# First stage of a two-layer trunk: three products and the low-rank features side by side by k-tile, in place of one output after another

## The chip, the cores and the metric

The kernel runs on one core of a Trainium2 chip. The metric is device time in microseconds; the number compared is the median of several runs.

## The reference

A streaming encoder takes 256 frames of a prompt and 32 frames of a sample, 288 tokens of 2048 features in float32, through two layers. Layer 0 is a mix of retention heads and gated linear attention heads (GLA), layer 1 is band attention; each is followed by a convolutional feed-forward block. Only the very beginning matters here:

```python
h = rmsnorm(x, p['norm_mix_g'][l])          # x * gain / rms, the rms over 2048 features of a token
z = jnp.einsum('btd,de->bte', h, w_in)       # 56 x 128 outputs, and 16 more: lo
qa, ka, va, ga, qb, kb, vb, gb, lo = jnp.split(z, cuts, axis=-1)
...
log_a = jax.nn.log_sigmoid(lo @ gate_w2 + gate_b) / GLA_GATE_TAU
```

The first GLA head needs its key, query and values (parts of kb, qb, vb) and the gates, which come out of the 16 low-rank features lo.

## The kernel before, in words

Features lie on the 128 partitions and the 288 tokens along the free dimension; a k-tile is 128 of the 2048 input features, so there are 16. Each float32 operand is split in two parts of a shorter type (a high part, h, and the low remainder, l), and a product is three TensorE passes per k-tile: wh with xh (L79), wh with xl (L80), wl with xh (L81). One output tile of 128 features is therefore 48 matmuls of 128x288. The rms factor R of a token is not multiplied into x; outputs are multiplied by R when they are read out of PSUM. So products can begin before R is known, and R is needed by whoever reads them.

`weights` (L50) loads 8 k-tiles of one output through SP's queue, ScalarE casts the high part (L57) and VectorE subtracts (L58). There are four buffers for w and three each for wh and wl. `gain_in` (L135) makes xh on ScalarE (L138) and xl on VectorE (L139) from x and the norm's gain.

`start` (L230) is the first stage. `first_project` (L83) loads x in four pieces and makes the key's product k0 while they arrive. Then come the low-rank features: their 16 columns of weights (wlo, loaded through POOL's queue) are split, both parts stand side by side in the columns of one tile, and two matmuls per k-tile (L251, L252) give them. Then q0 is made, `first_squares` (L99) sums the squares of x in the place of x, and `norm_stat` (L156) works out R: L164 sums over the partitions with ones, VectorE and ScalarE take the inverse root (`rsqrt`, with a table load of ScalarE for the root), L172 puts it on a diagonal (rd), L175 spreads it on all partitions, and L178 copies R out of PSUM. `ab_mixer` then multiplies lo by R (L404), and `gates` multiplies it with w2 (L416). The products that follow are v0 and v1 (the two value tiles) and the first gate tile.

The order on each engine is that of the built program: a scheduler settles it when the kernel is built, by the order of the code and its own estimate of when things are ready. Each engine then runs its list in order. SP's and POOL's loads are queues of their own on the same 16 DMA engines.

Of the kernel before, what the change touches and what calls it, by code (L numbers as in the profile page):

```python
# [33 lines left out]
class Trunk:  # L34
# [15 lines left out]
    def weights(self, src, n, lo=False):  # L50
        """n k-tiles of 128 rows: the float32 tile as the sum of two float32r tiles."""
        nc = self.nc
        w = self.wp.tile([P, WCH, P], F32, name="w", tag="w", bufs=4)[:, :n, :]
        h = self.wp.tile([P, WCH, P], F32R, name="wh", tag="wh", bufs=3)[:, :n, :]
        l = self.wp.tile([P, WCH, P], F32R, name="wl", tag="wl", bufs=3)[:, :n, :]
        nc.sync.dma_start(w, src)
        nc.scalar.copy(h, w)  # L57
        nc.vector.tensor_tensor(l, w, h.bitcast(F32), op=ALU.subtract)  # L58
        return h, l

    def project(self, src, xh, xl, nk, k0=0, chunks=None, part=None, ps=None):
        """PSUM [128 outputs, T]: the product over nk k-tiles of float32 operands split in two."""
# [20 lines left out]
    def first_project(self, src, x):  # L83
        """As project, while the input is loaded and the first norm's operands come about."""
        nc = self.nc
        ps = self.acc_ps.tile([P, 512], F32, name="acc", tag="acc")[:, :T]
        for c in range(0, KD, WCH):
            cuts = (0, 2, 8) if c == 0 else (8, 12, 16)
            for i, j in zip(cuts, cuts[1:]):
                nc.sync.dma_start(x[:, i:j, :], self.a["xT"][:, i:j, :])  # L90
                if j == cuts[1]:
                    h, l = self.weights(src[:, c : c + WCH, :], WCH)
            for j in range(WCH):
                k = c + j
                self.gain_in(k, 0)
                self.passes(ps, h[:, j, :], l[:, j, :], self.xh[k], self.xl[k], k == 0, k == KD - 1)
        return ps

    def first_squares(self, x):  # L99
        """The sum of squares, in the place of x."""  # L100
        nc, sq = self.nc, x
        for c in range(0, KD, 4):
            nc.scalar.activation(sq[:, c : c + 4, :], x[:, c : c + 4, :], AF.Square)
            if c:
                nc.vector.tensor_tensor(sq[:, 0:4, :], sq[:, 0:4, :], sq[:, c : c + 4, :], op=ALU.add)
        nc.vector.tensor_tensor(sq[:, 0:2, :], sq[:, 0:2, :], sq[:, 2:4, :], op=ALU.add)
        nc.vector.tensor_tensor(sq[:, 0, :], sq[:, 0, :], sq[:, 1, :], op=ALU.add)
        self.ssq = sq[:, 0, :]
# [8 lines left out]
    def rsqrt(self, out, ms_ps, inv_n, p=P, n=T, tag="rs"):  # L117
        """out = (ms_ps * inv_n + eps) ** -0.5"""
# [11 lines left out]
    def norm_in(self, k, n):  # L130
        """x[k] is final: its split product with the gain of norm n, and its square."""
        self.gain_in(k, n)
        self.square_in(k)
# [22 lines left out]
    def norm_stat(self):  # L156
        """R [128, T]: each token's 1 / rms, on all partitions; worked out with tokens on partitions."""
# [55 lines left out]
    def chain(self, heads, front, tail):  # L213
        """Heads as generators of steps. A head's steps after its first few take turns with the next one's
        first, so that its later products find their operands ready."""
# [10 lines left out]
    def out_start(self, w, chunks):  # L226
        """The first halves of out_proj's first sums, which the last head is not part of."""
        self.started = [self.project(w[m], self.bh, self.bl, KD, chunks=chunks, part=0) for m in range(2)]

    def start(self, pool):  # L230
        """The first norm, and the layer's first products beside it."""
        nc, a = self.nc, self.a
        w = a["w_in"]
        x_in = self._one(pool, "x_in", [P, KD, T])
        wlo = self._one(pool, "wlo", [P, KD, RANK], a["w_lo"])
        self.x = [x_in[:, k, :] for k in range(KD)]
        k0 = self.first_project(w[KB], x_in)
        # The gate's low-rank features: both parts of the weights side by side in one tile's columns
        # (their sum is taken in the product with w2, which stands twice).
        lo_ps = self.acc_ps.tile([P, 512], F32, name="acc", tag="acc")[:, :T]  # L240
        for c in range(0, KD, WCH):
            h = self.wp.tile([P, WCH, P], F32R, name="wh", tag="wh", bufs=3)
            nc.gpsimd.memset(h.bitcast(F32)[:, :, 2 * RANK :], 0.0)
            src = wlo[:, c : c + WCH, :]
            nc.scalar.copy(h[:, :, :RANK], src)
            nc.vector.tensor_tensor(
                h[:, :, RANK : 2 * RANK], src, h[:, :, :RANK].bitcast(F32), op=ALU.subtract
            )
            for j in range(WCH):
                k = c + j  # L250
                nc.tensor.matmul(lo_ps, lhsT=h[:, j, :], rhs=self.xh[k], start=k == 0, stop=False)  # L251
                nc.tensor.matmul(lo_ps, lhsT=h[:, j, :], rhs=self.xl[k], start=False, stop=k == KD - 1)  # L252
        q0 = self.input_product(w[QB])
        self.first_squares(x_in)
        self.ident = self.const("ident", [P, P], F32, a["ident"])
        self.norm_stat()
        return k0, q0, lo_ps

    def out_proj(self, w, n, chunks):
        """x += o @ w, and the next norm's start."""  # L260
# [83 lines left out]
    def head_out(self, pool, o, gates, hd, g):  # L344
        """Gated, normalised head output into the split operands of w_out; o: two PSUM tiles."""
# [18 lines left out]
    def to_tokens(self, pool, feats, name, width, scale=None, bufs=1):  # L364
        """[128 tokens, 3, width] from feature-major [128, T] tiles."""
# [22 lines left out]
    def ab_mixer(self, pool, k0, q0, lo_ps):  # L388
# [19 lines left out]
        def gates():  # L408
            """log sigmoid of the gates, tokens on partitions (its 1/16 is in the level matrices)."""
# [18 lines left out]
        def ret(hd):  # L428
# [9 lines left out]
            self.gla_head(pool, hd, w, la, lvl, masks, eyem, hg, (k0, q0, gates) if hd == 0 else None)  # L438
# [10 lines left out]
    def gla_head(self, pool, hd, w, la, lvl, masks, eyem, hg, first):  # L449
# [6 lines left out]
        v = [self.scaled(pool, self.input_product(w[VB + 2 * hd]), "v0")]  # L456
        if first:
            first[2]()
# [5 lines left out]
        # E[:, l]: decays to and from the middle of each token's block of level l. Slot 7: level 256  # L464
        # (tile 0 before, tile 1 behind the middle), and from the sample's start; slot 8: to the end.
# [31 lines left out]
        # Scores, transposed: each pair of tokens belongs to the one level whose middle parts them.  # L497
# [66 lines left out]
        # States.  # L564
# [89 lines left out]

    def att_head(self, pool, hd):
# [8 lines left out]
        # Keys stand in reversed order: the bias of query p and key column c is rel[c0 + p + c].  # L664
# [21 lines left out]
        # Tokens on partitions: the sample's, then the prompt's second and first 128.  # L686
# [27 lines left out]
        # Probabilities with keys on partitions: the first 128 and the second of the prompt's  # L714
        # (p0, p1), beside them the cache's two halves, and the sample's own (p2).
# [26 lines left out]
def _tiles(w):  # L742
    """[K, M] -> [M/128, 128, K/128, 128]: one output tile's rows, contiguous by partition."""
# [4 lines left out]
def _cols(v):  # L748
    """[..., N] -> [128, ..., N/128]: features on partitions."""
# [111 lines left out]
```

## Time and profile before

| | us |
|---|---|
| median of 3 runs | 2762.46 |
| lowest, highest | 2761.59, 2763.56 |
| span of the profiled execution (its own time: the profile gives none beside it) | 2760.1 |
| TensorE busy in the span | 2732.1 |
| start of the first product (L79) | 7.10 |
| start of L164 (sum of squares over partitions) | 30.39 |
| start of L416 (low-rank features with w2) | 39.64 |

In a row of the timeline the first number is the start in us from the span's start, the second the duration; then engine, line, operation, output and inputs with their shapes, and in brackets the idle time ahead of it and what ended it. PE is TensorE, PEld its weight load, DVE VectorE, ACT ScalarE. A 48-matmul product takes about 6.3 us. A duration of a matmul is longer than the distance to the next one, since matmuls overlap.

### The profile page before, as it was taken

To read this page: it belongs to the slowest core of one execution; us is meant where nothing else is said; L and a number is where in the kernel's file an instruction comes from. 1 tells how busy PE (TensorE), PEld (TensorE's weight loads), DVE (VectorE), ACT (ScalarE), POOL (GpSimd) and SP (SyncE) were. 2 spreads that over 40 slices of the span, in tenths; PEclk is the share of its full clock that TensorE was granted. 3 is DMA by queue.
4 is the path that set the end of the run, shared out by engine and by line. 5 is a ranking of instruction groups with operands and counts; after the bars stand their busy time and mean duration, and the time that the engine had idled before them with its cause. 6 is when DMAs were issued, how large, how long until landed. Compare 5 with 4: busy or idle time off the path is not lost.

```text
span 2760.1 us, 49198 instructions
## 1 busy us (share of the span) xinstructions
PE 2732.1 (99%) x20340; PEld 2686.5 (97%) x20340; DVE 1572.3 (57%) x2536; ACT 1123.9 (41%) x1538; POOL 126.5 (5%) x440
## 2 busy tenths in 40 slices
PE   8999999999999999999999999999999999999997
PEld 7999999999999999999999999999999999999997
DVE  6566555666665456665555555556666544666544
ACT  7444343443343333334444333344333333433443
POOL 1000000000000000000011111100000000000000
PEclk9999999999999999999999999999999999999999
DMA  5334444545555555555555555544555555555553
GB/s 198 117 131 142 152 157 149 192 162 166 168 167 161 168 168 165 167 168 162 166 182 170 166 165 165 163 156 162 166 165 166 162 167 168 168 166 166 163 167 125
DMA packets 126546, 448.84 MB, mean 163 GB/s; under 512 B 15562, under 2 KB 15754, under 8 KB 126320
## 3 DMA queue, kind: packets, MB, share of 16 engines
q1 hardware_dynamic: 119520, 427.15, 48.6%
q0 software_dynamic: 6656, 18.49, 2.1%
q8 instruction: 159, 2.61, 0.4%
q14 instruction: 67, 0.55, 0.1%
q10 hardware_dynamic: 144, 0.04, 0.0%
HBM read 435.22 MB, written 10.40 MB: 161 GB/s over the span
## 4 chain that ended last, share of the span: by engine, by line
PE 97%; ACT 1%; DVE 1%; DMA 1%; issue 0%; SPq 0%; DVEq 0%; ACTq 0%
PE acc L80 31%; PE acc L79 30%; PE acc L81 30%; PE mm L520 1%; DMA x_in<-in_xT 0%; PE mm L372 0%; PE mm L643 0%; ACT wh L57 0%; PE mm L682 0%; PE mm L685 0%; PE mm L734 0%; PE mm L681 0%; DVE wl L58 0%; DVE y L334 0%; PE mm L738 0%
## 5 line engine op out<-in xcount | busy, mean ns | idle before, releaser
L57 ACT CAST wh<-w 128x1024 fp32r<-128x1024 f32 (+1 forms) x816 | 843.7, 1034 | 1505.9 <-PE acc L80 1209.0
L58 DVE TENSOR_TENSOR wl<-w,wh 128x1024 fp32r<-128x1024 f32 (+1 forms) x816 | 981.0, 1203 | 761.7 <-ACT wh L57 761.4
L79 PE MATMUL acc<-xh,wh 128*128 128x288 f32 x4480 | 1323.0, 295 | 8.6 <-ACT wh L57 7.7
L81 PE MATMUL acc<-xh,wl 128*128 128x288 f32 x4480 | 1323.5, 295 | 1.3 <-DVE wl L58 1.3
L80 PE MATMUL acc<-xl,wh 128*128 128x288 f32 x4480 | 1324.0, 296 | 0.0
L79 PEld LDWEIGHTS acc<-xh,wh 128*128 128x128 f32 x4480 | 843.2, 188 | 13.3 <-ACT wh L57 7.9
L81 PEld LDWEIGHTS acc<-xh,wl 128*128 128x128 f32 x4480 | 842.6, 188 | 2.8 <-DVE wl L58 2.1
L80 PEld LDWEIGHTS acc<-xl,wh 128*128 128x128 f32 x4480 | 843.0, 188 | 2.0 <-issue 1.0
L79 PE MATMUL acc<-bh,wh 128*128 128x288 f32 x1920 | 567.1, 296 | 0.4 <-ACT wh L57 0.4
L80 PE MATMUL acc<-bl,wh 128*128 128x288 f32 x1920 | 566.3, 295 | 0.0
L81 PE MATMUL acc<-bh,wl 128*128 128x288 f32 x1920 | 565.0, 294 | 0.0
L79 PEld LDWEIGHTS acc<-bh,wh 128*128 128x128 f32 x1920 | 360.1, 188 | 1.3 <-ACT wh L57 0.6
L81 PEld LDWEIGHTS acc<-bh,wl 128*128 128x128 f32 x1920 | 361.2, 188 | 0.0
L80 PEld LDWEIGHTS acc<-bl,wh 128*128 128x128 f32 x1920 | 360.3, 188 | 0.1
L298 DVE SCALAR_TENSOR_TENSOR gc<-gp,convp,gc 128x290 f32<-128x290 f32 x176 | 91.3, 519 | 3.2
L304 DVE TENSOR_TENSOR v<-acc,R 128x288 f32<-128x288 f32 x88 | 40.3, 458 | 87.8 <-PE acc L81 87.8
L289 DVE TENSOR_TENSOR gp<-acc,R 128x256 f32<-128x256 f32 x88 | 37.5, 426 | 88.3 <-PE acc L81 88.3
L291 POOL COPY conv_out<-gp 128x2 f32<-128x2 f32 x88 | 16.4, 187 | 1312.7 <-DVE gp L289 1312.7
L114 ACT CAST bh<-v 128x288 fp32r<-128x288 f32 x88 | 38.1, 433 | 15.3 <-DVE v L306 15.3
L296 DVE TENSOR_SCALAR gc<-gp,convp 128x290 f32<-128x290 f32 x88 | 38.0, 432 | 9.5
L305 DVE TENSOR_TENSOR v<-v,sg 128x256 f32<-128x256 f32 x88 | 37.5, 426 | 9.9 <-DVE v L304 0.9
L115 DVE TENSOR_TENSOR bl<-v,bh 128x288 fp32r<-128x288 f32 x88 | 39.8, 452 | 0.7 <-ACT bh L114 0.7
(256 smaller groups left out, 1188.2 us busy)
## 6 DMA issues: line engine op xcount, KB each, us to landing
w<-in_w_ffn_up SPq DMA_DIRECT2D x352, 512.0 KB, 3.7
w<-in_w_ffn_down SPq DMA_DIRECT2D x128, 512.0 KB, 3.7
w<-in_w_in SPq DMA_DIRECT2D x112, 512.0 KB, 3.8
w<-in_w_qkv SPq DMA_DIRECT2D x96, 512.0 KB, 3.9
w<-in_w_ffn_down SPq DMA_DIRECT2D x64, 384.0 KB, 3.2
w<-in_w_out_ab SPq DMA_DIRECT2D x32, 512.0 KB, 3.8
w<-in_w_out_att SPq DMA_DIRECT2D x32, 512.0 KB, 3.8
x<-in_xT SPq DMA_DIRECT2D x4, 576.0 KB, 6.1
```

What stands on the lines that cost most here:

```text
L57: nc.scalar.copy(h, w)
L58: nc.vector.tensor_tensor(l, w, h.bitcast(F32), op=ALU.subtract)
L79: nc.tensor.matmul(ps, lhsT=h, rhs=xh, start=first, stop=False)
L80: nc.tensor.matmul(ps, lhsT=h, rhs=xl, start=False, stop=False)
L81: nc.tensor.matmul(ps, lhsT=l, rhs=xh, start=False, stop=last)
L114: self.nc.scalar.copy(h, v)
L115: self.nc.vector.tensor_tensor(l, v, h.bitcast(F32), op=ALU.subtract)
L289: nc.vector.tensor_tensor(gp[:, 2 : TP + 2], g[:, :TP], self.R[:, :TP], op=ALU.mult)
L296: nc.vector.tensor_scalar(gc, gp[:, 0:W], cw[:, 0:1], cw[:, 3:4], op0=ALU.mult, op1=ALU.add)
L298: nc.vector.scalar_tensor_tensor(gc, gp[:, w : w + W], cw[:, w : w + 1], gc, op0=ALU.mult, op1=ALU.add)
L304: nc.vector.tensor_tensor(v, u, self.R, op=ALU.mult)
L305: nc.vector.tensor_tensor(v[:, :TP], v[:, :TP], s[:, :TP], op=ALU.mult)
```

## The change

`first_products` replaces `first_project`, the loop for the low-rank features, q0's product and `first_squares`. It loads x and the weights of three outputs (query, key and first value tile of the first GLA head) in nine chunks: k-tiles 0 and 1 alone, then pairs. Per chunk there is one load of x and one of weights; the weights of the three outputs stand in one tile of 128 x 3 x n x 128, so one cast and one subtraction serve all three. Each k-tile is then multiplied for the three outputs and, from the second chunk on, for the low-rank features. wlo is loaded by SP behind the second chunk's weights and split into one tile for all 16 k-tiles. The squares of a chunk are taken one chunk later. All four accumulators are held at once. Ahead of everything stand eight 128x128 matmuls of ones with ones, whose result is not used, and a Square on one column of ones, which brings ScalarE's first table load with it. The value tile v0 is no longer made in `gla_head`.

```diff
+    def first_products(self, src, x, wlo, lo_h):
+        nc = self.nc
+        n_out = src.shape[1]
+        ps = [self.acc_ps.tile([P, 512], F32, name="acc", tag="acc")[:, :T] for _ in range(n_out + 1)]
+        cuts = (0, 1, 2, 4, 6, 8, 10, 12, 14, 16)
+        chunks = list(zip(cuts, cuts[1:]))
+
+        def square(i, j):
+            nc.scalar.activation(x[:, i:j, :], x[:, i:j, :], AF.Square)
+            if i > 1:
+                nc.vector.tensor_tensor(x[:, 0 : j - i, :], x[:, 0 : j - i, :], x[:, i:j, :], op=ALU.add)
+
+        for _ in range(8):
+            nc.tensor.matmul(self.mm()[:, :P], lhsT=self.ones, rhs=self.ones, start=True, stop=True)
+        for c, (i, j) in enumerate(chunks):
+            n = j - i
+            nc.sync.dma_start(x[:, i:j, :], self.a["xT"][:, i:j, :])
...
+            w, h, l = tile("w", F32, 4), tile("wh", F32R, 3), tile("wl", F32R, 3)
+            nc.sync.dma_start(w, src[:, :, i:j, :])
+            if c == 1:
+                nc.sync.dma_start(wlo, self.a["w_lo"])
+            for k in range(i, j):
+                self.gain_in(k, 0)
+                if k == i:
+                    nc.scalar.copy(h, w)
+                    nc.vector.tensor_tensor(l, w, h.bitcast(F32), op=ALU.subtract)
+                for o in range(n_out):
+                    self.passes(
+                        ps[o], h[:, o, k - i, :], l[:, o, k - i, :], self.xh[k], self.xl[k], k == 0, k == KD - 1
+                    )
+            if c == 1:
+                nc.vector.tensor_copy(lo_h[:, :, :RANK], wlo)
+                nc.vector.tensor_tensor(
+                    lo_h[:, :, RANK : 2 * RANK], wlo, lo_h[:, :, :RANK].bitcast(F32), op=ALU.subtract
+                )
+            for k in range(0 if c == 1 else i, j) if c else ():
+                nc.tensor.matmul(ps[-1], lhsT=lo_h[:, k, :], rhs=self.xh[k], start=k == 0, stop=False)
+                nc.tensor.matmul(ps[-1], lhsT=lo_h[:, k, :], rhs=self.xl[k], start=False, stop=k == KD - 1)
+            if c:
+                square(*chunks[c - 1])
+        square(*chunks[-1])
+        nc.vector.tensor_tensor(x[:, 0, :], x[:, 0, :], x[:, 1, :], op=ALU.add)
+        self.ssq = x[:, 0, :]
+        return ps
...
     def start(self, pool):
+        nc.scalar.activation(self.R[:, :1], self.ones[:, :1], AF.Square)
         x_in = self._one(pool, "x_in", [P, KD, T])
-        wlo = self._one(pool, "wlo", [P, KD, RANK], a["w_lo"])
+        wlo = self._one(pool, "wlo", [P, KD, RANK])
         self.x = [x_in[:, k, :] for k in range(KD)]
-        k0 = self.first_project(w[KB], x_in)
...
-        q0 = self.input_product(w[QB])
-        self.first_squares(x_in)
+        lo_h = self._one(pool, "lo_h", [P, KD, P], None, F32R)
+        nc.gpsimd.memset(lo_h.bitcast(F32)[:, :, 2 * RANK :], 0.0)
+        src = w[QB : VB + 1 : KB - QB].rearrange("o p k m -> p o k m")
+        q0, k0, v0, lo_ps = self.first_products(src, x_in, wlo, lo_h)
...
-        v = [self.scaled(pool, self.input_product(w[VB + 2 * hd]), "v0")]
+        v = first[2] if first else self.input_product(w[VB + 2 * hd])
+        v = [self.scaled(pool, v, "v0")]
```

What stands on TensorE's list at the end of the first stage before: the sums over partitions (L164) come behind q0's last passes, and v0's product begins right behind them; xh and xl are numbered by buffer.

```order
L80 MATMUL acc<-xl_101,wh 128x288
L81 MATMUL acc<-xh_85,wl 128x288
L164 MATMUL mm<-ones,x_in 96x1 [waits DVE_49]
L164 MATMUL mm<-ones,x_in 96x1 x2
L79 MATMUL acc<-xh_70,wh 128x288 [waits Activation_49]
L80 MATMUL acc<-xl_86,wh 128x288
```

In the middle of v0's product stands the spreading of R (L175), behind 25 of its passes; the other 23 follow, and L416 after them.

```order
L81 MATMUL acc<-xh_77,wl 128x288
L79 MATMUL acc<-xh_78,wh 128x288 [waits Activation_49]
L175 MATMUL mm<-rd,ones 128x96 [waits DVE_49] x3
L80 MATMUL acc<-xl_94,wh 128x288
L81 MATMUL acc<-xh_78,wl 128x288
```

The same place on TensorE after the change (L188 is the old L164, L199 the old L175, L430 the old L416, and L125 and L126 are the low-rank features): the three steps now follow one another, and v1's product comes behind them.

```order
L125 MATMUL acc<-xh_85,lo_h 128x288
L126 MATMUL acc<-xl_101,lo_h 128x288
L188 MATMUL mm<-ones,x_in 96x1 [waits DVE_49,PE_49]
L188 MATMUL mm<-ones,x_in 96x1 x2
L199 MATMUL mm<-rd,ones 128x96 [waits DVE_49,PE_49]
L199 MATMUL mm<-rd,ones 128x96 [waits DVE_49] x2
L430 MATMUL mm<-w_501,lo 128x512 [waits DMASW2_49,DVE_49,PE_49]
L430 MATMUL mm<-w_501,lo 128x512 [waits PE_49]
L430 MATMUL mm<-w_501,lo 32x512 [waits PE_49]
L79 MATMUL acc<-xh_70,wh 128x288 [waits Activation_49]
```

On ScalarE, the end of the stage after the change: the last chunk's cast (L113), the squares (L93), between them the two casts of the level matrices (lvl, which the decays use later), three casts of the next products' weights (L57), and then the table load and the root of the norm (L148).

```order
L113 CAST wh<-w 128x768 [waits DMAHW3_49,PE_49]
L93 ACTIVATE x_in<-x_in 128x576 [waits DVE_49]
L411 CAST lvl<-w 128x1024 [waits DMAHW4_49]
L411 CAST lvl<-w 128x128 [waits DMAHW5_49]
L93 ACTIVATE x_in<-x_in 128x576 [waits DVE_49,Activation_49]
L57 CAST wh<-w 128x1024 [waits DMAHW6_49,PE_49]
L57 CAST wh<-w 128x1024 [waits DMAHW7_49,PE_49]
L57 CAST wh<-w 128x1024 [waits DMAHW0_49,PE_49,Activation_49]
L148 ACT_TABLE_LOAD
L148 ACTIVATE rsq<-rv 96x3 [waits DVE_49]
L202 COPY R<-mm 128x288 [waits PE_49]
```

Before, the last square stood ahead of the two casts of the level matrices, and three casts of weights stood between those and the root as well.

On TensorE's list within a pair, the first three rows of the fifth chunk (k-tiles 6 and 7) stand like this after the change, so that the third pass of the first output asks for the low part at once:

```order
L79 MATMUL acc<-xh_76,wh 128x288 [waits Activation_49]
L80 MATMUL acc<-xl_92,wh 128x288 [waits DVE_49]
L81 MATMUL acc<-xh_76,wl 128x288 [waits DVE_49]
L79 MATMUL acc<-xh_76,wh 128x288
L80 MATMUL acc<-xl_92,wh 128x288
```

What moved: before, a product's passes for one output ran through 8 k-tiles on one pair of wh and wl; now a pair of k-tiles serves three outputs, and each chunk waits for its own cast and subtraction. From L430 on, the rows of TensorE, ScalarE, VectorE, POOL and SP are the same as before from L416 on.

More of the change, by code (lines that the diff above doesn't have):

```diff
@@ L81, in passes @@
         nc.tensor.matmul(ps, lhsT=l, rhs=xh, start=False, stop=last)
-    def first_project(self, src, x):
+    def first_products(self, src, x, wlo, lo_h):
         nc = self.nc
[L86 to L94, printed above, removed]
-                self.gain_in(k, 0)
-                self.passes(ps, h[:, j, :], l[:, j, :], self.xh[k], self.xl[k], k == 0, k == KD - 1)
-        return ps
@@ L99, in first_squares @@
[L99 to L108, printed above, removed]
+        n_out = src.shape[1]
@@ new lines, in first_products @@
+        for c, (i, j) in enumerate(chunks):
+            n = j - i
+            nc.sync.dma_start(x[:, i:j, :], self.a["xT"][:, i:j, :])
+            tile = lambda tag, dt, bufs: self.wp.tile([P, WCH, P], dt, name=tag, tag=tag, bufs=bufs)[
+                :, : n_out * n, :
+            ].rearrange("p (o k) m -> p o k m", o=n_out)
+            w, h, l = tile("w", F32, 4), tile("wh", F32R, 3), tile("wl", F32R, 3)
[3 more added lines that the diff above has]
+            for k in range(i, j):
+                self.gain_in(k, 0)
+                if k == i:
[15 more added lines that the diff above has]
+                square(*chunks[c - 1])
@@ L233, in start @@
         w = a["w_in"]
+        nc.scalar.activation(self.R[:, :1], self.ones[:, :1], AF.Square)
         x_in = self._one(pool, "x_in", [P, KD, T])
-        wlo = self._one(pool, "wlo", [P, KD, RANK], a["w_lo"])
+        wlo = self._one(pool, "wlo", [P, KD, RANK])
         self.x = [x_in[:, k, :] for k in range(KD)]
-        k0 = self.first_project(w[KB], x_in)
[L240 to L252, printed above, removed]
-        q0 = self.input_product(w[QB])
-        self.first_squares(x_in)
+        lo_h = self._one(pool, "lo_h", [P, KD, P], None, F32R)
+        nc.gpsimd.memset(lo_h.bitcast(F32)[:, :, 2 * RANK :], 0.0)
+        src = w[QB : VB + 1 : KB - QB].rearrange("o p k m -> p o k m")
+        q0, k0, v0, lo_ps = self.first_products(src, x_in, wlo, lo_h)
         self.ident = self.const("ident", [P, P], F32, a["ident"])
         self.norm_stat()
-        return k0, q0, lo_ps
+        return k0, q0, v0, lo_ps
     def out_proj(self, w, n, chunks):
@@ L386, in scaled, with ab_mixer @@
         return z
-    def ab_mixer(self, pool, k0, q0, lo_ps):
+    def ab_mixer(self, pool, k0, q0, v0, lo_ps):
         nc, a = self.nc, self.a
@@ L437, in ab_mixer @@
         heads = [
-            self.gla_head(pool, hd, w, la, lvl, masks, eyem, hg, (k0, q0, gates) if hd == 0 else None)
+            self.gla_head(pool, hd, w, la, lvl, masks, eyem, hg, (k0, q0, v0, gates) if hd == 0 else None)
             for hd in range(H_GLA)
@@ L455, in gla_head @@
         yield
-        v = [self.scaled(pool, self.input_product(w[VB + 2 * hd]), "v0")]
+        v = first[2] if first else self.input_product(w[VB + 2 * hd])
+        v = [self.scaled(pool, v, "v0")]
         if first:
-            first[2]()
+            first[3]()
         v.append(self.scaled(pool, self.input_product(w[VB + 2 * hd + 1]), "v1"))
```

## The prediction

> **What bounds the kernel now.** I read the page first, the shares of the span and the chain that ended last.
>
> ```profile
> span 2760.1 us, 49198 instructions
> PE 97%; ACT 1%; DVE 1%; DMA 1%; issue 0%; SPq 0%; DVEq 0%; ACTq 0%
> ```
>
> TensorE sets the time nearly everywhere, so an edit pays only where TensorE waits. The diff touches the first 42 us alone, and there TensorE waited for this (line, releaser, total us, times, longest):
>
> ```profile
> PE acc L79 <- ACT wh L57: 7.7, 2, 7.1
> PE mm L175 <- DVE rd L172: 1.3, 1, 1.3
> PE acc L81 <- DVE wl L58: 1.1, 2, 0.7
> PE acc L79 <- ACT xh L138: 0.9, 1, 0.9
> ```
>
> The 7.1 us is the start: no product before input and weights are loaded and cast. That sum of waits is what can be won; the timeline shows where each lies.
>
> ```profile
> 3.94 1.28 ACT L138 ACT_TABLE_LOAD   x1 [3.94 <-DMA x_in<-in_xT]
> 6.00 1.04 ACT L57 CAST wh<-w 128x1024 fp32r<-128x1024 f32 x1 [0.23 <-DMA w<-in_w_in]
> 7.10 0.61 PE L79 MATMUL acc<-xh,wh 128*128 128x288 f32 x1 [7.10 <-ACT wh L57]
> ...
> 13.51 0.44 PE L80 MATMUL acc<-xl,wh 128*128 128x288 f32 x1
> 13.74 0.38 PE L81 MATMUL acc<-xh,wl 128*128 128x288 f32 x1
> 13.96 0.30 PE L79 MATMUL acc<-xh,wh 128*128 128x288 f32 x1
> 14.10 0.29 PE L80 MATMUL acc<-xl,wh 128*128 128x288 f32 x1
> ...
> 14.40 1.05 ACT L57 CAST wh<-w 128x1024 fp32r<-128x1024 f32 x1 [0.85 <-DMA w<-in_w_in]
> ```
>
> Up to 13.7 us products start 0.23 us apart, then 0.13: a slow stretch costs 0.1 a product, some 23 products long. The norm's chain comes after it:
>
> ```profile
> 30.39 0.59 PE L164 MATMUL mm<-ones,x_in 128*96 128x1 f32 x6
> 33.09 1.28 ACT L124 ACT_TABLE_LOAD   x1
> 34.39 0.20 ACT L124 ACTIVATE rsq<-rv 96x3 f32<-96x3 f32 x1
> 34.62 0.17 DVE L125 RECIPROCAL ry<-rsq 96x3 f32<-96x3 f32 x1 [0.29 <-ACT rsq L124]
> 35.41 0.62 DVE L172 TENSOR_SCALAR rd<-ident,rn 96x96 f32<-96x96 f32 x3
> 35.73 0.91 PE L175 MATMUL mm<-rd,ones 96*128 96x96 f32 x6 [1.33 <-DVE rd L172]
> 36.67 0.40 ACT L178 COPY R<-mm 128x288 f32<-128x288 f32 x1 [1.15 <-PE mm L175]
> 37.11 0.45 DVE L404 TENSOR_TENSOR lo<-acc,R 32x288 f32<-32x288 f32 x1
> 39.64 2.95 PE L416 MATMUL mm<-w,lo 33*128 33x512 f32 x6
> 42.76 0.29 PE L80 MATMUL acc<-xl,wh 128*128 128x288 f32 x1
> 49.91 0.30 PE L80 MATMUL acc<-xl,wh 128*128 128x288 f32 x1
> ```
>
> The last two rows lie 54 products apart: (49.91 - 42.76)/54 = 0.132 us each, which all sums below use. Between L164 and L416 TensorE did v0's 48 products, so of the 9.25 us only the wait before L175 was idle.
>
> **What is compared.** From the gates' product (L416 before, L430 now) on, every engine's order is the same, so the change is worth the difference between the two starts of that product: 39.64 us before. Ahead of it stand the same 176 products (three outputs of 48, 32 for the low-rank features), 176 x 0.132 = 23.2 us.
>
> **The start.** SP now brings one k-tile of input (0.147 MB) and one of weights (three outputs, 0.197 MB) where it brought 0.295 and 0.524. The old first two landed at 3.94 and 6.00, so 0.344 MB lie at 3.94 + 2.06 x 0.049/0.524 = 4.1. The cast of 384 columns follows. Forms of such work, min/median/max:
>
> ```profile
> L138 ACT ACTIVATE xh<-x_in,gains x16: 518/521/535, 5.2 to 17.7; 128x288 fp32r<-128x288 f32 x16
> L139 DVE SCALAR_TENSOR_TENSOR xl<-x_in,gains,xh x16: 508/510/519, 5.8 to 18.8; 128x288 fp32r<-128x288 f32 x16
> L103 ACT ACTIVATE x_in<-x_in x4: 1148/1158/1166, 18.5 to 23.6; 128x1152 f32<-128x1152 f32 x4
> L106 DVE TENSOR_TENSOR x_in<-x_in x1: 757/757/757, 27.0 to 27.0; 128x576 f32<-128x576 f32 x1
> L57 ACT CAST wh<-w x816: 835/1052/1057, 6.0 to 2734.7; 128x1024 fp32r<-128x1024 f32 x150, 128x768 fp32r<-128x768 f32 x14
> L58 DVE TENSOR_TENSOR wl<-w,wh x816: 952/1225/1228, 7.1 to 2735.6; 128x1024 fp32r<-128x1024 f32 x150, 128x768 fp32r<-128x768 f32 x14
> ```
>
> From 0.84 (768) and 1.05 (1024), 384 columns are about 0.5: first real product at about 5.0 instead of 7.10. The moved table load (1.28) runs while x is still on its way, and the eight constant products end about when the data come: both cost nothing, the cover being the 3.9 us of load; at the slow spacing above, the constants would at worst reach past 5.0 by some tenths, which the next part's load wait swallows.
>
> **The load.** DMA is full for 15 us:
>
> ```profile
> 0.00:5.00 5.00, 0.00 (x0) 0.00 (x0) 0.46 (x2) 1.05 (x1) 3.94 (x13) 1.00 0.60 172
> 5.00:10.00 5.00, 2.18 (x6) 1.48 (x6) 2.17 (x3) 2.24 (x4) 2.16 (x6) 1.00 1.02 370
> 10.00:15.00 5.00, 4.29 (x18) 3.79 (x18) 3.52 (x8) 4.12 (x9) 1.44 (x3) 1.00 1.03 377
> ```
>
> (last three columns: granted clock, DMA share, GB/s.) That is 0.86 MB by 5 us, 2.71 by 10, 4.60 by 15. The stage is now nine chunks: k-tiles 0, 1, then pairs. A pair costs TensorE 22 products, 2.9 us; its 0.29 MB of input and 0.39 of weights take 1.8 us alone, but early on POOL's 1.07 MB of constants (ident, masks, w2, state, cos, sin, decays, by their shapes) share the engines. The 0.13 MB of wlo move from POOL's queue to SP's, behind the second chunk; they are counted below, and the low-rank products of the first k-tiles that wait for them stand ahead of the third chunk, which is later still. So the load binds first and TensorE later. The last chunk to be waited for is the fifth: through it SP brings 2.88 MB, and with POOL's and the gains 4.0 MB are due by 10 + 1.29/0.377 = 13.4. The old second weight tile, due by the same reckoning at 13.6 (4.06 MB), was cast at 14.40, 0.8 later; so these land at 14.2. Then cast 0.84, low part 0.95, hand-overs 0.1: 16.1. The third product of that chunk needs the low part; 108 remain: 14.3 us. The stage ends at 30.4; I take T = 30.5 for its end.
>
> Can the other engines follow? Per pair ScalarE has 2 x 0.52 + 0.84 + a square of 576 columns, between 0.4 and 1.16 and about 0.7 by width: 2.6 us. VectorE has 2 x 0.51 + 0.95 + 0.76 = 2.7. Both are under 2.9, VectorE barely.
>
> **Short rows.** Weight rows of 4 KB become 512 B and 1 KB: 384 packets a transfer instead of 128. The only SP transfer with rows of 512 B before is the tail of the level matrices, in 0.2 us at 19.0 and at 19.4:
>
> ```profile
> DMA packets 46, 0.04 MB, mean 197 GB/s; under 512 B 11, under 2 KB 40, under 8 KB 46
> DMA packets 17, 0.01 MB, mean 72 GB/s; under 512 B 3, under 2 KB 15, under 8 KB 17
> ```
>
> Ends: 0, the bytes alone; or 46 packets per 0.2 us as a ceiling, with POOL's share on top: 2688 packets to the fifth chunk, 11.7 us, + 2.8 us, from 2.6 us on, + 0.8: 17.9 instead of 14.2, +3.7 us. The second row is the last of a transfer draining, a rate no engine asked to exceed. I take 0.1 (the rounding of T): most rows are 1 and 2.3 KB, and DMA read 370 GB/s in the stretch with POOL's short rows too. The Trainium skill's "DMA: Bandwidth & Descriptors", "Why small descriptors are slow (HBM only)", speaks against the change: about 3 cycles per packet beside 32-byte beats, 35 for 32 at 1 KB, 19 for 16 at 512 B; estimated by that page, this is 0.6 us more on T and a gain of 3.4 instead of 4.0. No row here has such a transfer under load.
>
> **The norm's chain, now bare.** TensorE has nothing between L188, L199 and L430, where v0's products stood. Squares: ScalarE puts the two casts of the level matrices ahead of the last, but runs up to three chunks ahead of TensorE, so the sum is there before T. After T: L188 0.59; then VectorE's first step. ScalarE first casts the third weight tile of the next products, whose buffer the last chunk frees at about T - 0.5: until T + 0.55; table load 1.28, root 0.2: T + 2.1. From the reciprocal (34.62) to lo's end (37.11 + 0.45) took 2.94: L430 at T + 5.1 = 35.6. Of this 3.6 us are idle (5.1 less 0.59 and 0.91), a new wait that takes 2.3 more than the old 1.33. Behind L199 on TensorE stand L430 and v1's products; nobody else needs them sooner.
>
> **Sum.** Start -2.1; the stage's own waits and slow products (7.10 to 39.64 less 23.2, less 1.5 for L164 and L175: 7.8) become 2.3 (30.5 - 5.0 - 23.2) and 3.6: -1.9. Together 35.6 - 39.64 = -4.0 us. Span 2760.1 -> 2756.1; the median of the runs (2762.46) stands 2.4 above this span, so 2758.4. Runs of this kernel can tell about 0.2%, 5.5 us, from no change; this is below it.
>
> **Rivals.** (a) The loads never bind: T = 5.0 + 23.2 = 28.2, L430 at 33.3, -6.3, 2756.1, just over 0.2%. For it: smaller transfers need not finish as unevenly as the 0.8 us I carried over. Against: 2.71 MB by 10 us is only about three chunks beside POOL's. (b) The wait falls on a slow stretch again: after an idle 2.5 us TensorE may go back to 0.23 us. Place: L199, L430 and what follows; price up to the 6.6 us of the old stretch (7.10 to 13.74) at half rate, 3.3 us: 2761.7. Against: the 1.33 us before L175 brought none. By the Trainium skill ("TensorE: Matmul & The Clock Gate", "What's actually happening") the clock falls after an idle window of about 3.4 us, longer than either gap here; no row shows a gap that long, and by it (b) fails. (c) Short rows make SP's load the bound, and the kernel slower: at T = 34.5 the gain is gone, that is 2688 packets in 14.8 us, 180 per us; at T = 40 it loses 5.5, at 127 per us (the fifth chunk at 24.5). The draining row's 85 per us would give 31.6 us, T = 50.5, 2778. Against: 230 per us was seen. (d) VectorE sets the pace: 0.1 us of waiting at each of four steps makes 3.1 a pair, +1 us: 2759.4, inside my range.
>
> **Chances.** Forecast, with (d): 60%, own range 2757 to 2760. (a) 18%; (b) or short rows up to the ceiling 15%, 2760 to 2764; (c) 7%. Faster by over 0.2%: 18%; within: 75%; slower: 7%. The range goes from (a), 2756.0, to 2762.6, leaving out (c) and the far end of (b).
>
> **What would show it.** First real L79 near 5 us; waits of TensorE on the casts until the fifth chunk, none after; stage end near 30.5; a wait of about 2.6 us on rd before L199 and 1 us on lo before L430; L430 near 35.6. Wrong, if the fifth chunk's weights land after 18, if VectorE's queue holds TensorE in the pairs, or if the level matrices come so late that the last square is behind T.

## Result: 5.5 us slower, and the profile after

| | before | after |
|---|---|---|
| median of 12 runs each on one chip, us | 2762.42 (2761.59 to 2763.74) | 2767.97 (2767.26 to 2770.14) |
| ratio, 95% interval | | 1.002 [1.0012, 1.0028] |
| span of the profiled run, us | 2760.1 | 2768.4 (the run itself 2770.14) |

The forecast was 2758.4 with a range to 2762.6; the time lies 5.4 us above that range. The profiled run after is the longest of its twelve: eight of them lie at 2767.3 to 2768.2, and four at 2769.1 to 2770.1. The trace below therefore shows about 2 us more of loss than the median has.

The page's head, span and chain, of the kernel after:

```profile
span 2768.4 us, 49265 instructions
PE 98%; ACT 1%; DVE 1%; DMA 0%; issue 0%; SPq 0%; DVEq 0%; ACTq 0%
```

TensorE's waits in the first 60 us after (total us, times, longest):

```profile
PE acc L79 <- ACT wh L113: 3.9, 2, 2.6
PE mm L199 <- DVE rd L196: 2.8, 1, 2.8
PE mm L430 <- issue: 1.0, 1, 1.0
```

The 7.1 us at the start are gone from this list, since the constant products now run there; the first real product starts at 4.96, as forecast. What remains is waits for the casts of two chunks (1.31 us before the second's products at 8.21, 2.55 us before the third's at 14.20) and two waits in the norm. The timeline after shows where they lie (start, us, engine, line; in brackets the idle time ahead and who ended it):

```profile
4.96 0.61 PE L79 MATMUL acc<-xh,wh 128*128 128x288 f32 x1
...
13.31 0.83 ACT L113 CAST wh<-w 128x768 fp32r<-128x768 f32 x1 [2.68 <-DMA w<-in_w_in]
14.20 0.61 PE L79 MATMUL acc<-xh,wh 128*128 128x288 f32 x1 [2.55 <-ACT wh L113]
14.60 0.44 PE L80 MATMUL acc<-xl,wh 128*128 128x288 f32 x1
14.84 0.44 PE L79 MATMUL acc<-xh,wh 128*128 128x288 f32 x1
...
36.63 0.59 PE L188 MATMUL mm<-ones,x_in 128*96 128x1 f32 x6
38.57 0.20 ACT L148 ACTIVATE rsq<-rv 96x3 f32<-96x3 f32 x1
40.00 1.38 PE L199 MATMUL mm<-rd,ones 96*128 96x96 f32 x6 [2.78 <-DVE rd L196]
42.39 5.59 PE L430 MATMUL mm<-w,lo 33*128 33x512 f32 x6 [1.02 <-issue]
47.91 0.61 PE L79 MATMUL acc<-xh,wh 128*128 128x288 f32 x1
...
63.37 0.39 PE L486 MATMUL mm<-lvl,lah 128*128 128x512 f32 x1
```

The decays' first product (L486) is the old L471, which stood here before:

```profile
55.74 0.39 PE L471 MATMUL mm<-lvl,lah 128*128 128x512 f32 x1
```

It is 7.63 us later, and the span is 8.3 us longer, so nearly all of the loss lies ahead of it. The gates' product itself starts only 2.75 us later than before (42.39 against 39.64). The cast at 13.31 is the third chunk's (k-tiles 2 and 3); it waited for the load. Products from 14.20 on are 0.24 us apart again. L430 takes 5.59 us where L416 took 2.95.

The granted clock explains those two. Stretches of the trace after (start:end, length, then busy us and instructions of PE, PEld, DVE, ACT, POOL; then the clock, DMA share and GB/s):

```profile
6.07:9.48 3.41, 2.10 (x14) 1.71 (x14) 1.71 (x4) 1.39 (x3) 1.37 (x4) 1.00 1.01 313
9.48:12.89 3.41, 2.01 (x11) 1.35 (x10) 0.95 (x2) 0.96 (x2) 0.49 (x1) 1.00 1.05 348
12.89:19.72 6.83, 5.52 (x23) 5.52 (x24) 5.12 (x9) 5.76 (x11) 0.00 (x0) 0.50 1.05 343
19.72:36.79 17.07, 17.07 (x132) 17.07 (x131) 14.06 (x21) 12.68 (x21) 0.00 (x0) 1.00 0.79 257
36.79:40.20 3.41, 0.63 (x8) 0.57 (x8) 2.56 (x9) 1.95 (x3) 0.00 (x0) 1.00 0.65 211
40.20:53.85 13.65, 12.63 (x37) 8.21 (x37) 4.51 (x11) 9.02 (x15) 0.00 (x0) 0.50 0.10 35
```

The clock is halved twice, for 6.83 us and for 13.65 us, which are two and four times 3.41. Each fall follows a stretch of 3.41 us in which TensorE was busy for 2.01 and 0.63 us. Before, the clock rose once, at 13.9 us, and stayed up until 2748 us.

In the prediction's terms the way to the decays is: forecast -4.0; stage end 36.63 instead of 30.5, +6.1; chain 5.76 instead of 5.1, +0.7; L430 5.59 instead of 2.95, +2.6; and v1's products, slow from 47.91 to 53.85, about 24 x 0.1 = +2.4. Together that is +7.8, against 7.63 measured.

### The profile page after: what moved, and what is told of

Its sections match the earlier page's. It is cut to its first block, busy times and chain, and to the rows that moved or that the text cites. A ratio compares the mean times of both kernels' runs of the same rounds, so it can differ in the third digit from the quotient of the medians.

```text
span 2768.4 us, 49265 instructions
## 1 busy us (share of the span) xinstructions
PE 2742.6 (99%) x20356; PEld 2695.3 (97%) x20356; DVE 1572.7 (57%) x2542; ACT 1125.2 (41%) x1545; POOL 125.8 (5%) x438
## 4 chain that ended last, share of the span: by engine, by line
PE 98%; ACT 1%; DVE 1%; DMA 0%; issue 0%; SPq 0%; DVEq 0%; ACTq 0%
PE acc L80 31%; PE acc L79 31%; PE acc L81 31%; PE mm L535 1%; DMA w<-in_w_in 0%; PE mm L386 0%; PE mm L658 0%; PE mm L697 0%; PE mm L700 0%; PE mm L749 0%; PE mm L696 0%; ACT wh L57 0%; DVE y L348 0%; PE mm L430 0%; PE mm L753 0%; ACT L492 0%
## 5 line engine op out<-in xcount | busy, mean ns | idle before, releaser
L57 ACT CAST wh<-w 128x1024 fp32r<-128x1024 f32 (+1 forms) x810 | 837.5, 1034 | 1505.3 <-PE acc L80 1222.5
```

## Experiments

The loss was read as three things: weights that come late, TensorE's clock, and the order on ScalarE in the norm. Differences below are between medians of 10 or 11 runs (the changed kernel's 2767.97 is from 12). The medians of the kernel before in the three sets were 2762.35 (long_rows, warm_tail, warm_head, v1_cover), 2762.87 (late_const, no_dummy, v1_long, best) and 2762.99 (late_long, root_first, gates128, repaired). Against its own set's before, a run of the second or third set stands about half a us better than these differences say.

Each kernel has one trace, and traces differ where the code does not. In the seven traces that share the first stage's loads (after, warm_tail, warm_head, v1_cover, no_dummy, root_first, gates128) the third chunk is cast between 12.16 and 13.31 us, and the norm's sums start between 33.73 and 36.63.

### One loss at a time

**long_rows.** Weights of the three outputs side by side in memory:

```diff
-            nc.sync.dma_start(w, src[:, :, i:j, :])
+            nc.sync.dma_start(w, src[:, i:j])     # src = w_first [P, KD, 3, P]
```

> The first stage's weights are laid out in memory with the three outputs side by side for each k-tile, so that each load writes one piece of 512 B to 3 KB per partition instead of three of 512 B to 1 KB; values, order and sizes stay. Theory (the short pieces bring the third chunk late and open the gap in which the clock falls): its weights are cast at about 10.5 us instead of 13.3, no product runs at 0.24 us before the norm, the norm's sums start at about 31 us instead of 36.6, and the kernel gains 5 to 6 us on the changed one (about 2762, level with before). Rival (the loads are as late with long pieces, since the bytes ahead in the queues set it): cast at 13 us, norm's sums at 36 to 37, no change.

Measured: 2766.16, 1.8 us less than the change; ratio to before 1.0014 [1.0005, 1.0023]. The third chunk was cast at 10.74, no clock fell in the stage, and the sums came at 32.95. So the pieces' length does bring the weights late, but it is not all of the stage's miss (30.5 forecast). The gain of time is a third of what was expected: the norm's wait behind it grew to 4.3 us, and the clock fell there as before.

DMA in two stretches, after and then long_rows (last columns: clock, DMA share, GB/s):

```profile
5.00:10.00 5.00, 3.69 (x21) 3.30 (x22) 2.20 (x5) 1.97 (x5) 2.92 (x8) 1.00 0.96 300
10.00:15.00 5.00, 2.29 (x10) 1.63 (x10) 1.77 (x3) 2.32 (x5) 0.00 (x0) 0.79 1.05 344
```

```profile
5.00:10.00 5.00, 3.94 (x22) 3.30 (x20) 1.61 (x4) 1.51 (x4) 2.94 (x8) 1.00 1.02 363
10.00:15.00 5.00, 3.85 (x22) 3.10 (x22) 3.43 (x6) 3.94 (x7) 0.00 (x0) 1.00 1.04 374
```

The DMA engines are about as busy, but move 300 and 344 GB/s with short pieces (512 B and 1 KB), and 363 and 374 with long ones (1.5 and 3 KB); before, it was 370 and 377.

**warm_tail.** Products whose results nobody uses, in the norm's two waits:

```diff
+        for _ in range(11 if self.fill else 0):
+            nc.tensor.matmul(fill, lhsT=self.ones, rhs=self.ssq[:, :P], start=True, stop=True)
...
+        for _ in range(4 if self.fill else 0):
+            nc.tensor.matmul(fill[:, :m], lhsT=self.ones[:m, :], rhs=d[:, 2, :], start=True, stop=True)
```

> Eleven products with ones after the norm's sums and four after its broadcast, all results unused, fill most of TensorE's two waits in the first norm; no wait gets shorter. Theory (the loss behind the norm is the clock that falls in these waits): the gates' product takes 2.95 us instead of 5.59, v1's products 0.13 instead of 0.24, and the kernel gains 5 us (4.5 to 5.5) on the changed one. Rival (the products after the norm are slow for another reason, operands or memory): no change, or up to 1 us lost by the added products.

Measured: 2766.18, 1.8 us less, not 5; ratio 1.0012 [1.0004, 1.0021]. Its norm and what follows, in stretches:

```profile
36.04:39.45 3.41, 3.09 (x28) 2.93 (x28) 2.75 (x10) 2.02 (x3) 0.00 (x0) 1.00 0.62 208
39.45:42.86 3.41, 3.29 (x18) 2.14 (x18) 2.28 (x7) 0.92 (x2) 0.00 (x0) 1.00 0.43 147
42.86:46.27 3.41, 3.41 (x8) 1.35 (x8) 0.08 (x1) 3.38 (x7) 0.00 (x0) 0.50 0.00 0
```

The first wait is filled and the clock holds through it. It falls one stretch later all the same, at 42.86, though TensorE was busy for 3.29 of those 3.41 us. That stretch holds products over 96 rows and the gates' product over 33. This was not expected, and led to gates128 below.

**warm_head.** The same ahead of the third chunk's products:

```diff
+            for _ in range(11 if c == 2 else 0):
+                nc.tensor.matmul(fill, lhsT=self.ones, rhs=x[:, 2, :P], start=True, stop=True)
```

> Eleven products with ones, results unused, on the third input tile as soon as it has landed, ahead of the third chunk's products, fill the wait for that chunk's weights. Theory (the clock falls in that wait): no products at 0.24 us between 14 and 20 us, the norm's sums start at about 34.1 us instead of 36.6, and the kernel gains 2.5 us. Rival (the clock falls there by its own grid whatever TensorE does, or the later chunks' loads bind anyway): the norm's sums stay at 36 to 37 and nothing is gained.

Measured: 2768.19, no change; ratio 1.002 [1.0011, 1.0029]. In its trace no clock falls ahead of the norm, and the sums start at 34.59, as the theory has it. The time does not follow, and the runs spread from 2766.17 to 2770.12. The fall at 12.89 in the changed kernel's trace is therefore not what its median suffers from. Five traces share the first stage's code (after, warm_tail, v1_cover, root_first, gates128): their sums start at 36.63, 35.84, 33.73, 35.50 and 35.48, with the clock halved there for 6.8, 2 x 3.4, 3.4, 2 x 3.4 and 3.4 us.

**v1_cover.** Work in place of waits: v1's product goes into the norm.

```diff
+        v1 = self.mm()[:, :T]
+        part = lambda i: self.project(w[VB + 1], self.xh, self.xl, KD, chunks=(0, WCH), part=i, ps=v1)
+        self.norm_stat(part)      # part(0) ahead of the root, part(1) ahead of R's copy
```

> The second value product of the first head (48 products, 6.3 us) is moved into the norm's two waits, half of it between the norm's sums and its broadcast and half between the broadcast and the gates' product; its sum goes to a bank of the other PSUM pool, since the first four sums hold all banks of its own. Theory (bare waits of 3.8 us and the clock that falls in them are the loss behind the norm): the first decays come 8 to 9 us earlier against the norm's sums than in the changed kernel, and the kernel gains 8 us (7 to 9): about 2760. Rival (only the clock counts, the waits return elsewhere, at the gates' chain, which then stands bare): 5 us. Rival (neither): no change.

Measured: 2760.58, 7.4 us less; ratio 0.9993 [0.9984, 1.0002], so level with before. The decays come 17.3 us behind the sums instead of 26.7. The gates' product, with its clock up:

```profile
33.73 0.59 PE L188 MATMUL mm<-ones,x_in 128*96 128x1 f32 x6
41.71 2.95 PE L434 MATMUL mm<-w,lo 33*128 33x512 f32 x6
```

The norm's waits and the clock in them are the larger part of the loss. Some comes back later: the second part of the decays now waits 1.9 us for ScalarE at 55.80, and the clock falls there for 3.4 us.

**late_const.** GpSimd's large constants wait for the fifth k-tile:

```diff
+    def hold(self, t):
+        self.nc.gpsimd.tensor_copy(t, self.xh[4][:, :1].bitcast(F32))
...
+        self.hold(...)            # ahead of the loads of masks, st, cosR, sinR, dec
```

> GpSimd's five large loads of constants for later stages (masks, the first state, cos, sin, decays: 848 KB) wait for the split input of the fifth k-tile; all else as in the changed kernel. Theory (these loads share the DMA engines with the first chunks' weights and bring them late): the third chunk's weights are cast 1 to 2 us earlier than 13.3 us, the norm's sums start 2 to 3 us earlier than 36.6, and the kernel gains 2 to 3 us (about 2765). Rival (SP's own loads queued behind each other set the landings, and later chunks take the share that becomes free): cast at 12.5 to 13.5 and under 1 us gained.

Measured: 2768.59, no gain; ratio 1.0021 [1.0012, 1.0031]. The third chunk was cast at 10.43, 2.9 us earlier than in the trace of the change. The sums came at 34.49, no earlier than in other traces with the old loads: what was won at the third chunk was lost at the eighth, which TensorE now waited for. The norm's wait grew as well. Rows of both places, and TensorE's wait in the norm:

```profile
26.94 0.83 ACT L113 CAST wh<-w 128x768 fp32r<-128x768 f32 x1 [2.39 <-DMA w<-in_w_in]
27.83 0.41 PE L79 MATMUL acc<-xh,wh 128*128 128x288 f32 x1 [1.34 <-ACT wh L113]
36.40 1.04 ACT L57 CAST wh<-w 128x1024 fp32r<-128x1024 f32 x1 [2.87 <-DMA w<-in_w_in]
40.25 0.20 ACT L148 ACTIVATE rsq<-rv 96x3 f32<-96x3 f32 x1
```

```profile
PE mm L199 <- DVE rd L196: 6.6, 1, 6.6
```

The held constants are issued from 14.00 on and landed by 26.7, so they now share the engines with the stage's last chunks: the eighth chunk's weights, issued at 15.07, took 11.8 us to land. With these late, SP issues the next products' weights from 28.79 on instead of 26.99. Their casts stand ahead of the root on ScalarE and wait for their data, so the root runs 5.8 us behind the sums instead of 1.9.

**no_dummy.** The eight products with ones are taken out:

```diff
-        for _ in range(8):
-            nc.tensor.matmul(self.mm()[:, :P], lhsT=self.ones, rhs=self.ones, start=True, stop=True)
```

> The eight products with ones ahead of the first real one are taken out (one part of the change undone). Theory A (they raise the clock early, and what is gained by that reaches the end of the stage): the clock rises some 5 to 10 us later, the norm's sums start 1 to 2.5 us later, and the kernel loses 1 to 2.5 us on the changed one. Theory B (the loads of the first chunks bind, so that the early clock is lost in waits): the norm's sums move by under 0.5 us and no change.

Measured: 2767.77, no change; ratio 1.0019 [1.001, 1.0027]. The clock rose at 13.79 instead of 6.07. The sums came at 34.19, which lies among the traces with these loads, and R's broadcast (L199 after) at 39.50 against 40.00. Theory B holds for the time: here a clock that was up early, while TensorE waited for loads, was worth nothing.

### Losses together

**v1_long** is v1_cover and long_rows.

```diff
+            nc.sync.dma_start(w, src[:, i:j])
...
+        self.norm_stat(part)
```

> v1_cover and long_rows together. If the pieces' length and the norm's waits are separate losses, they add: the norm's sums at about 33, no fall of the clock before them, the first decays 17.3 us behind the sums as in v1_cover, and 1.5 to 2 us less than v1_cover (about 2759). If long pieces only paid by sparing a fall of the clock that not every run has, under 1 us.

Measured: 2759.14, 1.4 us less than v1_cover; ratio 0.9988 [0.9979, 0.9997]; sums at 31.86. The two add: each measured against its own set's before, v1_long stands 2.0 us below v1_cover.

**best** holds the constants too.

```diff
+            nc.sync.dma_start(w, src[:, i:j])
...
+        self.norm_stat(part)
...
+        self.hold(...)            # masks, st, cosR, sinR, dec
```

> v1_cover, long_rows and late_const together. Theory (DMA traffic of the first 15 us sets when the dense products begin): the norm's sums at 30.5 to 31.5 us and 2 us less than v1_long (about 2757). Rival (the clock's falls and the order of SP's loads set it): as v1_long, within 0.7 us.

Measured: 2757.54, 1.6 us less than v1_long and 5.3 less than before; ratio 0.9982 [0.9973, 0.999]. The sums came at 30.36. Held constants, worth nothing alone, pay when the pieces are long as well; late_long below shows the same with v1 left in place. This is the fastest kernel of the study. It still has the wait of 1.9 us in the decays:

```profile
30.36 0.59 PE L188 MATMUL mm<-ones,x_in 128*96 128x1 f32 x6
53.14 0.33 PE L498 MATMUL mm<-lvl,lah 128*128 128x128 f32 x1 [1.90 <-ACT E L504]
```

**late_long** is long_rows and late_const, with v1 left where the change has it.

```diff
+            nc.sync.dma_start(w, src[:, i:j])
...
+        self.hold(...)            # masks, st, cosR, sinR, dec
```

> long_rows and late_const together, v1's products left where the change has them. Theory (short pieces and GpSimd's constants are what brought the first stage's end from the forecast 30.5 us to 34 to 37): the norm's sums at 30.5 (30 to 31). For the time: if the earlier sums reach the end, 2764 (4 us less than the changed kernel); rival: the root of the norm stands on ScalarE behind the casts of v1's weights, which come by their loads and not by the sums, so that the wait in the norm grows by what the stage gains, and the time is 2766 to 2768.

Measured: 2764.32, 3.65 us less than the change; ratio 1.0004 [0.9995, 1.0013].

```profile
30.63 0.59 PE L188 MATMUL mm<-ones,x_in 128*96 128x1 f32 x6
35.00 1.57 PE L199 MATMUL mm<-rd,ones 96*128 96x96 f32 x6 [3.78 <-DVE rd L196]
37.58 5.59 PE L430 MATMUL mm<-w,lo 33*128 33x512 f32 x6 [1.01 <-issue]
```

```profile
10.00:15.00 5.00, 5.00 (x36) 4.58 (x35) 4.62 (x9) 5.00 (x10) 3.54 (x7) 1.00 1.04 401
```

The sums came at 30.63, where the forecast had the stage's end (30.5). DMA moved 401 GB/s from 10 to 15 us and TensorE did not wait there. The stage's miss is short pieces and GpSimd's constants together; the gain reaches the end. With the loads, the casts ahead of the root come earlier too (the last at 31.21 instead of 36.21). The norm's wait and the slow L430 are still there.

**root_first.** Casts of the next weights are made to wait for 1 / rms:

```diff
+        if self.held:
+            self.held -= 1
+            nc.vector.tensor_copy(h[: T // 3, 0, :1], self.rn[:, :1])
         nc.scalar.copy(h, w)
```

> In the changed kernel the casts of the three weight chunks behind the first stage are made to wait for the norm's 1 / rms, so that the root runs ahead of them on ScalarE; nothing else moves. Theory (the root waits behind casts that wait for loads or for a buffer): the root begins 0.8 us behind the sums instead of 1.9, the broadcast 2.2 to 2.6 us behind them instead of 3.4, and 1 to 1.5 us are gained; 6 us if the shorter wait (1.6 to 2 us) also spares the fall of the clock. Rival (the wait is the chain's own steps): broadcast at 3.4 and nothing gained.

Measured: 2767.03, 0.9 us less; ratio 1.0015 [1.0006, 1.0024], an interval that holds the change's own ratio. The root ran 0.8 us and the broadcast 2.25 us behind the sums, as expected. Most of it was given back: the first cast, let go by 1 / rms, now stands on ScalarE ahead of R's copy, and its subtraction (L61) on VectorE ahead of lo.

```profile
35.50 0.59 PE L191 MATMUL mm<-ones,x_in 128*96 128x1 f32 x6
36.32 0.20 ACT L151 ACTIVATE rsq<-rv 96x3 f32<-96x3 f32 x1 [5.57 <-DVE rv L150]
37.75 0.88 PE L203 MATMUL mm<-rd,ones 96*128 96x96 f32 x6 [1.66 <-DVE rd L200]
38.10 1.04 ACT L60 CAST wh<-w 128x1024 fp32r<-128x1024 f32 x1 [1.58 <-DVE wh L59]
39.05 0.39 ACT L206 COPY R<-mm 128x288 f32<-128x288 f32 x1
39.18 1.23 DVE L61 TENSOR_TENSOR wl<-w,wh 128x1024 fp32r<-128x1024 f32 x1 [1.03 <-ACT wh L60]
40.86 5.59 PE L435 MATMUL mm<-w,lo 33*128 33x512 f32 x6 [2.23 <-issue]
```

The gates' product starts 5.36 us behind the sums instead of 5.76, and the clock still fell.

**gates128.** warm_tail with more rows in the gates' product:

```diff
-        w2 = one("w2", [2 * RANK + 1, 512], a["w2"])
+        w2 = one("w2", [P, 512])
+        nc.vector.memset(w2, 0.0)
+        nc.gpsimd.dma_start(w2[: 2 * RANK + 1], a["w2"])
...
-        lo = one("lo", [2 * RANK + 1, T])
+        lo = one("lo", [P, T])
```

> warm_tail with the gates' product on 128 rows (the 95 rows added are zeros in the weights) in place of 33. Theory (a product over 33 rows counts as little activity, so that the clock falls in it although TensorE has no wait): the product takes 2.95 us instead of 3.96, v1's products 0.13 us from the start, and 3 us less than warm_tail (about 2763). Rival (rows don't matter, the clock fell for the 1 us of waits): as warm_tail, 2766.

Measured: 2764.10, 2.1 us less than warm_tail; ratio 1.0004 [0.9995, 1.0013].

```profile
38.45:41.86 3.41, 2.17 (x17) 1.89 (x16) 2.04 (x10) 0.46 (x2) 0.00 (x0) 1.00 0.81 257
41.86:45.28 3.42, 3.42 (x5) 0.89 (x5) 1.50 (x5) 1.76 (x2) 0.00 (x0) 0.50 0.03 13
45.28:48.69 3.41, 3.41 (x21) 2.54 (x20) 0.00 (x0) 3.38 (x7) 0.00 (x0) 1.00 0.00 0
```

The clock fell here too, at 41.86, behind a stretch with waits and products over 96 rows. But it rose again after one stretch, which held only the gates' product. With 33 rows the same product filled 43.61 to 47.02 after the change, and the clock stayed down. So TensorE's busy time is not all that counts: a product over 33 rows did less to bring the clock up than the same product over 128. How much less is not settled.

**repaired** is late_long, root_first, six and four fill products and the wider gates' product, with v1 left in place.

```diff
+            nc.sync.dma_start(w, src[:, i:j])
...
+        self.hold(...)            # masks, st, cosR, sinR, dec
...
+            nc.vector.tensor_copy(h[: T // 3, 0, :1], self.rn[:, :1])
...
+        for _ in range(6 if self.fill else 0): ...
...
+        w2 = one("w2", [P, 512])
```

> The changed kernel with its three found losses mended and v1's products left in place: long pieces and held constants (late_long), the root ahead of the casts (root_first), results-unused products in the norm's waits (six and four) and the gates' product on 128 rows. If the three are the whole miss, the sum of the prediction comes out: the norm's sums at 30.5, the gates' product at 35 to 35.6 and 2.95 us long, first decays at 51 to 52 (55.74 before), and the time 2758 (2757.5 to 2759). If something else holds the kernel up, 2760 or more.

Measured: 2758.63; ratio 0.9984 [0.9975, 0.9993].

```profile
30.82 0.59 PE L191 MATMUL mm<-ones,x_in 128*96 128x1 f32 x6
36.18 4.53 PE L444 MATMUL mm<-w,lo 128*128 128x512 f32 x6 [1.34 <-issue]
53.45 0.39 PE L507 MATMUL mm<-lvl,lah 128*128 128x512 f32 x1
```

The median is where the sum of the prediction lay (2758.4). Not every place is: in the traced run (2759.54) the clock still fell once, the gates' product came at 36.18 and took 4.5 us, and the decays came at 53.45, 2.3 us ahead of before instead of 4. It shows that these losses are the miss of the total, not that each term of the sum was right.

## Why the prediction was wrong

**The start: right.** First real product at 4.96 (5.0 forecast). The constant products and the table load cost nothing there. Without the constant products the time is the same, so they are worth nothing either. The moved table load was not tried by itself.

**The load: the step that failed first.** The sum held all bytes due by the fifth chunk to the old 377 GB/s and added one lag of 0.8 us: landed at 14.2. Those weights, issued at 6.75, took 11.2 us and landed at about 18.0 (from 16.7 on in the seven traces with these loads), so this term was 2.5 to 3.8 us too small; the far end is the ceiling that the prediction gave for short rows (17.9). The waits lay earlier besides: the third chunk's weights were ready for their cast at 13.31, and by then TensorE was so far behind that it did not wait for the fifth chunk at all (its cast began at 18.40 with no wait for data). Two things made the loads late. The rate sank to 300 and 344 GB/s with pieces of 512 B and 1 KB, where the prediction took 0.1 us for them between bounds of 0 and 3.7. And GpSimd's constants shared the engines just then; they were counted as bytes of a whole, which says nothing of who lands first. The fifth chunk's weights landed at 16.2 with long pieces (long_rows), at 15.0 with the constants held (late_const), and at 13.2 with both (late_long), where the stage ended at 30.63. By the Trainium skill, "DMA: Bandwidth & Descriptors", "Why small descriptors are slow (HBM only)", each packet costs about 3 cycles beside its 32-byte beats; an estimate from that is 9% more for pieces of 1 KB and 19% more for those of 512 B. The rate from 5 to 10 us is 17% below that with long pieces and from 10 to 15 us 8% below, so the trace agrees roughly. The 0.1 us taken was too little: long pieces brought the fifth chunk's landing forward by 0.5 to 1.8 us with the constants where they were, and by 1.8 us with them held.

**The clock: the rival that was set aside.** The sum put slow products behind the first stage at nothing, and took the start of the gates' product as the whole worth of the change because the order behind it is the same. The order was, the speed was not. Rival (b) named the place and the effect, and priced it at up to 3.3 us, for 6.6 us at half clock. The traced run was at half clock for 13.65 us and lost 2.6 + 2.4 us behind the norm, and some of its stage. It was dismissed for two reasons, and neither held. The first was that 1.33 us of wait before L175 had brought no fall. That wait was close to the limit; stretches of the kernel before, of v1_cover and of gates128, each on the grid of its own trace:

```profile
34.38:37.79 3.41, 2.08 (x17) 2.06 (x17) 3.03 (x10) 1.54 (x3) 0.00 (x0) 1.00 0.84 279
```

```profile
4.98:8.39 3.41, 1.92 (x11) 1.53 (x12) 1.36 (x3) 1.87 (x5) 2.24 (x7) 1.00 0.94 306
8.39:11.80 3.41, 3.41 (x16) 3.35 (x16) 1.85 (x5) 0.99 (x3) 0.70 (x2) 0.50 1.04 339
```

```profile
4.32:7.73 3.41, 1.99 (x12) 1.40 (x11) 1.22 (x3) 1.72 (x4) 2.60 (x9) 1.00 0.90 283
```

With 2.08 us of TensorE in 3.41 the clock stayed, and in gates128 with 1.99; with 1.92 it fell in v1_cover, where the longest wait was 1.28 us. The second reason was the Trainium skill, "TensorE: Matmul & The Clock Gate", "What's actually happening": the clock falls after an idle window of about 3.4 us. That section's length of the window agrees with the traces (3.41 us, on a grid that lies differently in each run). That a whole window must be idle does not.

**The norm's chain: nearly right, by luck.** The root's end was forecast at T + 2.1 and came at 38.77 - 36.63 = 2.14; the gates' product came at 5.76 instead of 5.1, since L199 (1.38 us) and what follows already ran at half clock. But the forecast tied the casts ahead of the root to a buffer alone. They wait for their loads as well: in late_const, where the loads are later, the root began at T + 5.8 instead of T + 1.9. An earlier end of the stage alone does not move it: in the trace of the change and in those of warm_tail, warm_head, gates128 and no_dummy the sums start anywhere from 34.19 to 36.63, and R's broadcast from 38.72 to 40.00.

**The other rivals.** (a) is out: the loads bound. (c) named short pieces as a way to be slower, with T = 34.5 as the break-even: they are a part of the miss, 1.8 us of the time, but the constants and the clock are more. Its later cases leave out the lag of 0.8 us that the first one counts, so 127 per us belongs to T near 40.8 and the draining row's rate to T near 51. (d) did not show: from 19.72 to 36.79 TensorE was busy without a gap. The prediction's "DMA is full for 15 us" also misreads its first row, where the share is 0.60; the sum used the bytes and is not touched.

Where it went, by the runs: of the 9.6 us between forecast and measurement, 3.65 are the first stage's loads (late_long; about half a us more against its own set's before). A further 5.7 are the norm's bare waits and the clock (late_long to repaired). v1_cover, which fills the same waits with work, wins 7.4 alone. How the 5.7 divide between the clock, the root's place and the waits is not settled: warm_tail, root_first and gates128 give 1.8, 0.9 and 2.1 more, and each leaves a fall of the clock behind.

## What to carry to other kernels

When a change strips the work that covered a short serial chain, price the chain's idle time and the slow products behind it, and look at how busy TensorE is in each few us rather than at the longest gap. When loads are regrouped, look at who else loads at that moment and at how long the pieces are, and then at the in-order queues behind: here ScalarE held the norm's root behind casts that waited for loads. A load that is held back takes its share of the engines later: held constants alone only made later chunks late (late_const), and paid once the pieces were long as well (late_long, best).

## What the runs showed of the hardware

The granted clock changes at multiples of 3.41 us. On that grid, stretches with products over 128 rows alone let it fall with 1.92 us of TensorE work (v1_cover), 1.96 (root_first) and 2.01 (after), and with less; it stayed up with 1.99 (gates128), 2.10 (after) and 2.30 (warm_head). So the limit lies near 2.0 us of 3.41, and these figures, in which a product's end is modelled, do not place it more finely. Stretches that also held products over 96 or 33 rows let it fall at 2.04 (repaired), 2.17 (gates128) and 3.29 us (warm_tail); one held at 2.08 (before). In v1_cover a longest wait of 1.28 us was enough, and the same first stage met such falls at different places in five traces. Once down, the clock came back after one full stretch of dense products over 128 rows, but not after a full one of a product over 33 rows.
